# Two gate tiles of a decoder block made in the input projection instead of between attention steps

## The chip, the cores and the metric

The kernel runs on one core of a Trainium2 chip. The metric is the device time of one execution in microseconds; lower is better. A core has TensorE (PE, matmuls into the PSUM banks), VectorE (DVE), ScalarE (ACT), GpSimd (POOL) and SyncE (SP, which issues nearly all DMAs here). Each runs its own instructions in order and waits for the others by semaphores.

## The reference

One layer of a decoder trunk on x of 1024 rows and 1024 channels, all in float32. Cut to what matters:

```python
h = rms_norm(x, norm_gain, 1e-6)
proj = einsum('bsd,de->bse', h, w_in)        # 1024 x 8456
(qa, ka, va, ga, qb, kb, vb, gb, qc, kc, vc, fc, gc, gm) = split(proj)
ya = rms_norm(diff_attention(qa, ka, va, lam), subln_gain) * (1 - lam_init)   # 4 heads, all keys before
yb = sliding_window_attention(qb, kb, vb, sinks)                              # 8 heads, window 128
yc = forgetting_attention(qc, kc, vc, cumsum(log_sigmoid(fc + b_forget)))     # 8 heads, all keys before
ua, ub, uc = (y * silu(g)) @ w_up            # for each of the three branches, 512 -> 1024
gates = sigmoid(gm.reshape(B, S, 3, D))      # three gates of 1024 channels
merged = gates[:, :, 0]*ua + gates[:, :, 1]*ub + gates[:, :, 2]*uc
out = rms_norm(x + merged @ w_o, final_gain)
```

The part that the change touches is `gm`: 3 x 1024 of the projection's columns, that is 24 tiles of 128 channels by 1024 rows, eight for each branch.

## The kernel before

Every number that a matmul reads is held as a rounded part and a rest (`hi` and `lo`, function `split`, L98 to L104), and a product is three matmuls: hi by hi, hi by lo, lo by hi (`mm3`, L106 to L111). A matmul has 128 x 128 weights and 512 columns (512 rows of x). One tile of 128 output channels over 1024 rows and 1024 inputs therefore costs 8 inner blocks x 2 halves of the rows x 3 = 48 matmuls when it is made directly, and two tiles 96. `strassen` (L162 to L215) makes two tiles together from seven products of 12 matmuls, 84 in all. For that it also needs sums of the weights (`comb`, L167 to L170, DVE) and sums of the products (DVE), and four combinations of the activations, which are made once (`t_part`).

The program has these stages, in order:

1. x is normalised and transposed, and the v columns are projected.
2. The input projection proper: one direct tile (`KB`), then a list `tiles` that is taken in pairs, each pair a call of `strassen` (L503 to L511). The list holds the q and k tiles of the three branches, the tiles of the silu gates, and those tiles of `gm` that are not named in `DIRECT`: `tiles += [... sigm(bi, d)) for bi in (0, 2, 1) for d in range(NK) if (bi, d) not in DIRECT]`. Such a tile goes through the sigmoid at once (`sigm`, L440 to L445: ACT at L443, a DMA to the scratch tensor `gmd` at L444).
3. Attention, 64 steps ("units"): 16 of the window branch (b), 32 of the forgetting branch (c), 16 of the differential branch (a). The last two are taken per head in groups of two row blocks, g = 3, 2, 1, 0, from long rows to short ones. PE's order here is the order in which the code is written (`manual_schedule`); the other engines' order is set by a scheduler. In step n PE makes the scores of unit n (L755 or L630), and between them the transposes (L676) and the products with v (L709 or L780) of unit n - 2. In between, for a unit, come: on DVE the masked scores and their row minimum (L757, L650), on ACT the exponential (L760, L656), on DVE a reciprocal (L658), on POOL the scaling of the row (L664; in branch a the sum of two rows, L840). A transposed tile goes out of PSUM by ACT (L682) and DVE (L683). Scores have two PSUM buffers, so a score waits for the row minimum of the score before last.
4. Between these pieces stand the *fillers* (`fillers`, L519 to L541): the tiles of `DIRECT`, made directly, three matmuls at a time (L531 to L533; I call three a slot), 16 slots a tile. Each piece of attention work has a cost c, and behind it `fill(c * rate[kind] / 0.65)` adds to an account from which whole slots are spent; `rate` is `FILL_B`, `FILL_C` or `FILL_A` by the branch. `FILL_0 = 28` slots stand ahead of the first score, and `FILL_END = 8` are kept for the end. A filler's weights are split on POOL (L103 and L104); its result goes raw to `gmd` (L537, L538). The last six tiles of `DIRECT` are made for the second half of the rows first. Once that is done, the buffers of those rows are free, and from that step on two pieces per step of branch b's gating are put in (`gate_load`, `gate`: L560, L567, L101, L104), eight gatings in all.
5. The up-projections in the order b, c, a with the gates (`up`, L1033 to L1048). A gate tile of `DIRECT` gets its sigmoid here (L1040). Then the output projection (again by `strassen`) and the last norm.

## Time and profile before

| | |
|---|---|
| median of three runs | 1188.73 us (1188.29 to 1191.81) |
| the profiled execution | 1184.62 us, span 1182.8 us |
| PE busy in the span | 1147.9 us (97%), 5787 matmuls seen |
| PE weight loads | 972.6 us (82%) |
| DVE, ACT, POOL busy | 815.4 (69%), 585.5 (50%), 693.8 us (59%) |
| input projection (first to last matmul of it) | 129.8 to 529.5 us |
| first 28 filler slots | 529.5 to 548.6 us |
| attention, from the first score to the last product | 548.6 to 962 us |
| up- and output projection | 962 to 1182.8 us |

Busy time of PE is to be read with care: a matmul's row lasts 0.39 us, but the next one starts 0.23 us later, so rows overlap, and a PE that is always busy need not be at its full pace. The pace is read from starts, in the timeline. What an engine waited for stands in brackets behind a row of the timeline, and summed up in the view of the waits.

### The profile page before, as it was taken

The numbers are of one execution on the slowest core, as the hardware profiler recorded it, in microseconds if no ns is written. First come the engines' busy times: TensorE is split into PE (matmuls) and PEld (weight loads), VectorE is DVE, ScalarE is ACT, GpSimd is POOL, SyncE is SP. The second block draws the span as 40 slices with busy tenths as digits, with TensorE's granted clock in tenths as the row PEclk, the third lists the DMA queues.
The fourth block names the chain that finished last, engine by engine and source line by source line (L and its number), as shares of the span: only waits on it lengthen the run. The fifth ranks groups of instructions, "written<-read, shape, count | busy, mean of one in ns | idle before, by whom it ended". The sixth has DMA issues, their size and how long they took to land. (4 is left out here: it accounts for less than half of the span.)

```text
span 1182.8 us, 18767 instructions
## 1 busy us (share of the span) xinstructions
PE 1147.9 (97%) x5787; PEld 972.6 (82%) x5787; DVE 815.4 (69%) x1655; ACT 585.5 (50%) x1255; POOL 693.8 (59%) x684
## 2 busy tenths in 40 slices
PE   7999999999999999998999999999998999999997
PEld 6999888888888888887888888888877878888775
DVE  7767767768687775322887767768677835664898
ACT  6432333433444444323886666667877842334423
POOL 5056656657667676454556665766767732477643
PEclk8999999999999999999999999999999999999999
DMA  7442266666856555349946466466668359798322
GB/s 242 155 153 91 103 209 230 233 213 198 266 185 205 166 164 161 99 117 247 258 117 194 133 191 183 134 176 172 176 205 234 121 163 337 271 345 306 129 107 107
DMA packets 184531, 221.70 MB, mean 187 GB/s; under 512 B 16280, under 2 KB 116712, under 8 KB 182640
## 3 DMA queue, kind: packets, MB, share of 16 engines
q1 hardware_dynamic: 184288, 219.99, 58.9%
q8 instruction: 46, 0.75, 0.3%
q14 instruction: 53, 0.43, 0.1%
q10 hardware_dynamic: 144, 0.52, 0.1%
HBM read 144.89 MB, written 75.56 MB: 186 GB/s over the span
## 5 line engine op out<-in xcount | busy, mean ns | idle before, releaser
L104 POOL TENSOR_TENSOR w_lo<-w_st,w_hi 128x512 fp32r<-128x512 f32 x130 | 173.4, 1340 | 108.5 <-ACT w_hi L101 89.4
L104 POOL TENSOR_TENSOR w_lo<-w_sf,w_hi 128x512 fp32r<-128x512 f32 x96 | 143.2, 1494 | 104.8 <-ACT w_hi L101 84.4
L109 PE MATMUL pm<-t,w_hi 128*128 128x512 f32 x320 | 126.3, 395 | 0.7 <-ACT w_hi L101 0.7
L111 PE MATMUL pm<-t,w_lo 128*128 128x512 f32 x320 | 126.3, 395 | 0.0
L110 PE MATMUL pm<-t,w_hi 128*128 128x512 f32 x320 | 126.0, 394 | 0.0
L630 PE MATMUL sc<-qk 128*128 128x512 f32 (+2 forms) x384 | 101.9, 356 | 3.7 <-DVE m L650 3.7
L683 DVE TENSOR_TENSOR pt<-tp,pt 128x512 fp32r<-128x512 f32 x102 | 70.1, 687 | 23.8 <-ACT pt L682 23.0
L169 DVE TENSOR_TENSOR w_sf<-w_st 128x512 f32<-128x512 f32 x40 | 47.7, 1193 | 43.5 <-DMA w_st<-in_w_in_dram 34.8
L630 PEld LDWEIGHTS sc<-qk 128*128 128x128 f32 x384 | 64.6, 189 | 15.3 <-DVE m L650 6.8
L101 ACT CAST w_hi<-w_sf 128x512 fp32r<-128x512 f32 x96 | 58.5, 613 | 35.4 <-PE pm L110 29.5
L109 PEld LDWEIGHTS pm<-t,w_hi 128*128 128x128 f32 x320 | 60.1, 188 | 14.9 <-ACT w_hi L101 1.1
L110 PEld LDWEIGHTS pm<-t,w_hi 128*128 128x128 f32 x320 | 60.1, 188 | 14.1
L111 PEld LDWEIGHTS pm<-t,w_lo 128*128 128x128 f32 x320 | 60.1, 188 | 14.1
L101 ACT CAST w_hi<-w_st 128x512 fp32r<-128x512 f32 x86 | 51.3, 615 | 37.6 <-PE pm L110 28.5
L682 ACT CAST pt<-tp 128x512 fp32r<-128x512 f32 x102 | 59.4, 582 | 20.4 <-PE tp L676 18.8
L423 ACT ACTIVATE qk_hi<-u 128x512 fp32r<-128x512 f32 x32 | 20.2, 633 | 94.2 <-DVE u L191 43.9
L664 POOL TENSOR_SCALAR e_c<-e_c,r 128x1024 f32<-128x1024 f32 (+3 forms) x64 | 47.9, 749 | 23.8 <-DVE r L658 20.0
L709 PE MATMUL y<-pt,v 128*128 128x256 f32 x336 | 55.4, 290 | 2.4 <-DVE pt L683 2.2
L656 ACT ACTIVATE e_c<-e_c,m 128x1024 f32<-128x1024 f32 (+3 forms) x64 | 49.9, 780 | 13.7 <-DVE m L650 12.8
L840 POOL TENSOR_TENSOR e_a<-e_a,e_a 128x896 f32<-128x896 f32 (+7 forms) x32 | 47.3, 1481 | 15.9 <-ACT e_a L839 15.8
L656 ACT ACTIVATE e_a<-e_a,m 128x896 f32<-128x896 f32 (+7 forms) x64 | 49.6, 775 | 13.3 <-DVE m L650 13.1
L1048 POOL TENSOR_TENSOR mt<-mt,row 128x512 f32<-128x512 f32 x28 | 39.5, 1426 | 24.7 <-DVE row L1047 24.6
(299 smaller groups left out, 3511.4 us busy)
## 6 DMA issues: line engine op xcount, KB each, us to landing
w_st<-in_w_in_dram SPq DMA_DIRECT2D x126, 256.0 KB, 3.4
qk<-qd SPq DMA_DIRECT2D x224, 128.0 KB, 3.1
wo<-wod SPq DMA_DIRECT2D x14, 1024.0 KB, 9.0
row<-gmd SPq DMA_DIRECT2D x48, 256.0 KB, 4.5
qd<-qk_hi SPq DMA_DIRECT2D x42, 256.0 KB, 4.1
qd<-qk_lo SPq DMA_DIRECT2D x42, 256.0 KB, 4.9
vd<-vt SPq DMA_DIRECT2D x24, 384.0 KB, 2.3
v<-vd SPq DMA_DIRECT2D x9, 1024.0 KB, 9.8
```

The lines of the kernel that those rows point to most:

```text
L101: first = nc.scalar.copy(hi, src)
L104: return first, eng.tensor_tensor(lo, src, hi.bitcast(F32), ALU.subtract)
L109: nc.tensor.matmul(ps, w[0][:, k, :], r[0][:, k, :], start=start and k == 0, stop=False)
L110: nc.tensor.matmul(ps, w[0][:, k, :], r[1][:, k, :], start=False, stop=False)
L111: nc.tensor.matmul(ps, w[1][:, k, :], r[0][:, k, :], start=False, stop=stop and k == n - 1)
L169: nc.vector.tensor_tensor(t, x, y, op)
L630: nc.tensor.matmul(ps[:, :n], q, kk[t][c][:, o:o + n], start=t == 0, stop=t == 1)
L656: nc.scalar.activation(e[:, :L], e[:, :L], AF.Exp, bias=m2, scale=-1.0, accum_out=den)
L664: nc.gpsimd.tensor_scalar(out=e, in0=e, scalar1=r, scalar2=1.0, op0=ALU.mult, op1=ALU.mult)
L682: nc.scalar.copy(pt[:, 0, a:], tp[:, a:])
L683: nc.vector.tensor_tensor(pt[:, 1, a:], tp[:, a:], pt[:, 0, a:].bitcast(F32), ALU.subtract)
L709: nc.tensor.matmul(y[:, :256], l_, r_, start=t == 0 and n == 0, stop=last and n == len(mms) - 1)
```

## The change

```diff
-DIRECT = [(0, d) for d in range(8)] + [(2, d) for d in (6, 7, 4, 5, 2, 3, 0, 1)]
+DIRECT = [(0, d) for d in range(2, 8)] + [(2, d) for d in (6, 7, 4, 5, 2, 3, 0, 1)]
 NLAST, GPART, NY, NSUM = 6, 2, 5, 8.0
 GATE_AT = {"b": (0, 1, 2, 3, 4, 4, 5, 5), "c": (1, 1, 2, 2, 3, 4, 5, 5)}
 FILL_END, FILL_Z = 8, 1.5
-FILL_0, FILL_B, FILL_C, FILL_A = 28, 0.8, 0.6, 0.75
+FILL_0, FILL_B, FILL_C, FILL_A = 28, 0.68, 0.51, 0.64
```

Gate tiles 0 and 1 of branch a leave `DIRECT`, and so enter the list `tiles` as one more pair for `strassen`, between the silu gates and the gate tiles of branch b. There are 224 filler slots in place of 256: 28 stand ahead of the first score as before, 37 in place of 44 in branch b's steps, 81 in place of 95 in branch c's, 70 in place of 81 in branch a's, and 8 at the end as before.

On PE, at the end of the projection: `t` are the combined activations, `h` the activations, `pm` and `pj` the PSUM tiles of the projection and of a filler. Before, the 20th pair is the last one, and the fillers begin behind it:

```order
L109 MATMUL pm<-t_1313,w_hi 128x512
L110 MATMUL pm<-t_1314,w_hi 128x512
L111 MATMUL pm<-t_1313,w_lo 128x512
L531 MATMUL pj<-h01h,w_hi 128x512
L532 MATMUL pj<-h01l,w_hi 128x512
L533 MATMUL pj<-h01h,w_lo 128x512
```

and now, at the same row of PE's list:

```order
L109 MATMUL pm<-t_1313,w_hi 128x512
L110 MATMUL pm<-t_1314,w_hi 128x512
L111 MATMUL pm<-t_1313,w_lo 128x512
L109 MATMUL pm<-h00h,w_hi 128x512
L110 MATMUL pm<-h00l,w_hi 128x512
L111 MATMUL pm<-h00h,w_lo 128x512
```

A pair of 84 matmuls more stands between the last combination product and the first filler.

On PE in branch c, from the last score of the third head's g = 3 unit (the first row, `sc` of 384 columns) to its first transposes (`tp`, four of them). Before:

```order
L630 MATMUL sc<-qk 128x384 x2
L531 MATMUL pj<-h01h,w_hi 128x512
L532 MATMUL pj<-h01l,w_hi 128x512
L533 MATMUL pj<-h01h,w_lo 128x512
L630 MATMUL sc<-qk 128x512 x2
...
L630 MATMUL sc<-qk 128x256 x2
L531 MATMUL pj<-h11h,w_hi 128x512
L532 MATMUL pj<-h11l,w_hi 128x512
L533 MATMUL pj<-h11h,w_lo 128x512
L676 MATMUL tp<-ident,e_c 128x128 x4
```

and now, the end of the same stretch:

```order
L709 MATMUL y<-ptz_5170,v 128x256 x4
L630 MATMUL sc<-qk 128x256 x2
L676 MATMUL tp<-ident,e_c 128x128 x4
L531 MATMUL pj<-h00h,w_hi 128x512
L532 MATMUL pj<-h00l,w_hi 128x512
```

The slot that stood ahead of the transposes now stands behind them; in this stretch there were three slots and there are two. So it is in four of the eight heads; in the other four there were two before, and there are two.

On DVE, where branch b's gating begins (`gate` L567, `yg_b` L104) among branch a's row minima (L650). Before, behind the last unit of the second head:

```order
L650 ISA e_a_10135,m<-sc,posA 128x256
L650 ISA m 128x1
L658 RECIPROCAL r<-den 128x1
L838 COPY dens<-den 128x1
L567 TENSOR_TENSOR gate<-gate 128x512
L658 RECIPROCAL r<-den 128x1
```

and now:

```order
L683 TENSOR_TENSOR ptz_5170<-tp,ptz_5170 128x384
L658 RECIPROCAL r<-den 128x1
L837 SCALAR_TENSOR_TENSOR r<-r,nlam,den 128x1
L567 TENSOR_TENSOR gate<-gate 128x512
L683 TENSOR_TENSOR pt<-tp,pt 128x512
L650 ISA e_a_10108,m<-sc,posA 128x128
```

Counted in scores from the first step of attention, the eight gatings stood behind scores 208, 211, 218, 228, 229, 234, 238 and 249, and now stand behind 204, 205, 208, 215, 227, 228, 232 and 238.

## Rows read from the trace of the kernel before

**Rows 1.** Windows by stage: stretch, busy time of each engine (instructions), clock, DMA, GB/s

```profile
129.80:529.50 399.70, 399.05 (x1729) 324.36 (x1728) 271.18 (x311) 157.49 (x275) 253.66 (x178) 1.00 0.58 183
548.60:575.00 26.40, 22.44 (x125) 19.02 (x124) 18.02 (x71) 18.40 (x61) 12.57 (x24) 0.94 0.91 256
575.00:625.00 50.00, 50.00 (x298) 43.53 (x297) 42.29 (x143) 41.38 (x130) 28.15 (x52) 1.00 0.60 170
625.00:800.00 175.00, 173.84 (x1084) 152.96 (x1083) 123.98 (x371) 113.21 (x253) 113.28 (x186) 1.00 0.58 167
800.00:875.00 75.00, 73.85 (x436) 63.13 (x434) 54.51 (x191) 57.48 (x127) 50.02 (x49) 1.00 0.62 183
875.00:962.00 87.00, 78.74 (x469) 65.80 (x468) 59.65 (x192) 66.27 (x152) 59.69 (x58) 1.00 0.55 164
962.00:1182.80 220.80, 210.77 (x912) 171.41 (x910) 155.78 (x216) 75.16 (x145) 108.66 (x76) 0.98 0.65 230
```

**Rows 2.** Timeline of PE (start, length), first matmuls of two successive pairs in the projection

```profile
393.75 0.39 PE L109 MATMUL pm<-h00h,w_hi 128*128 128x512 f32 x1
...
413.15 0.39 PE L109 MATMUL pm<-h00h,w_hi 128*128 128x512 f32 x1
```

**Rows 3.** Timeline of PE, two filler slots in branch c and what follows each

```profile
735.20 0.39 PE L531 MATMUL pj<-h11h,w_hi 128*128 128x512 f32 x1
...
735.90 0.63 PE L709 MATMUL y<-ptz,v 128*128 128x256 f32 x4
...
737.08 0.48 PE L531 MATMUL pj<-h11h,w_hi 128*128 128x512 f32 x1
...
737.86 0.63 PE L630 MATMUL sc<-qk 128*128 128x512 f32 x2
```

**Rows 4.** Waits of PE in attention, 548.6 to 962: us in total, times, longest

```profile
PE sc L630 <- DVE m L650: 3.7, 6, 2.6
PE sc L755 <- DMA qk<-qd: 3.4, 2, 2.3
PE y L709 <- DVE pt L683: 2.2, 1, 2.2
PE pj L867 <- POOL y L104: 1.5, 2, 1.0
...
PE tp L676 <- POOL e_c L664: 0.7, 2, 0.4
```

**Rows 5.** Timeline of PE, first steps of attention

```profile
553.17 0.77 PE L755 MATMUL sc<-kb,qk 128*128 128x256 f32 x2 [2.27 <-DMA qk<-qd]
553.74 0.63 PE L531 MATMUL pj<-h10h,w_hi 128*128 128x512 f32 x1
...
555.02 1.05 PE L755 MATMUL sc<-kb,qk 128*128 128x256 f32 x4
...
557.00 0.39 PE L531 MATMUL pj<-h10h,w_hi 128*128 128x512 f32 x1
```

**Rows 6.** Timelines of PE and POOL, the third head's g = 3 unit of branch c

```profile
677.36 0.40 PE L531 MATMUL pj<-h11h,w_hi 128*128 128x512 f32 x1
...
678.06 0.60 PE L676 MATMUL tp<-ident,e_c 128*128 128x128 f32 x4
676.25 1.02 POOL L664 TENSOR_SCALAR e_c<-e_c,r 128x896 f32<-128x896 f32 x1
```

**Rows 7.** Timeline of all engines around PE's longest wait in branch a

```profile
884.45 2.52 POOL L104 TENSOR_TENSOR w_lo<-w_st,w_hi 128x512 fp32r<-128x512 f32 x2
...
884.49 1.28 DVE L837 SCALAR_TENSOR_TENSOR r<-r,nlam,den 128x1 f32<-128x1 f32 x1
...
886.15 1.37 DVE L567 TENSOR_TENSOR gate<-gate 128x512 f32<-128x512 f32 x1
...
888.19 0.73 PE L630 MATMUL sc<-qk 128*128 128x512 f32 x2 [2.62 <-DVE m L650]
```

**Rows 8.** Groups of instructions: sigmoids of the direct gate tiles in the up-projection

```profile
L1040 ACT ACTIVATE row<-row 128x512 f32<-128x512 f32 x32 | 19.9, 631 | 35.2 <-DMA row<-gmd 33.7 <-DVE w_sf L169 0.9 <-POOL w_lo L104 0.6
```

## The prediction

> **What bounds the kernel now.** I read the windows by stage first, then PE's timeline inside the two stages that the change touches, then PE's waits there, and last the other engines around the longest wait. The windows show PE busy for 399.05 of the projection's 399.70 us, while DVE is at 271, POOL at 254 and ACT at 157 [rows 1]. That busy share alone proves little, since rows overlap; the starts do: the first matmuls of two successive pairs lie 413.15 - 393.75 = 19.40 us apart [rows 2], which over 84 matmuls is 0.231 us each, the spacing of matmuls that wait for nothing. The projection is bound by PE's own work.
>
> In attention PE is again busy nearly throughout in branch c (173.84 of 175 us, DVE 71%, POOL and ACT 65%), but the others come nearer in branch b (DVE 85%, ACT 83% of 575 to 625) and in the last stretch of branch a PE drops to 78.74 of 87 us while ACT is at 76% [rows 1]. The waits name what PE waits for: 3.7 us for row minima, 3.4 for the first query rows to land, 2.2 for one transposed tile from DVE, 1.5 for a split on POOL, 0.7 for scaled rows [rows 4]. So attention is bound by PE with little to spare: the fillers are what fills the time in which the chain from a score to its transposes runs. Whether a removed slot gives its time back depends on whether that chain was already late at its place.
>
> **The change part by part.** I add up against the profiled execution (1184.62 us, of which 1182.8 is the span; the rest lies outside it). The median of three is 1188.73, 4.1 us above, and I carry the difference over to the median.
>
> *Added in the projection: one pair.* 84 matmuls, by the distance of two pairs 19.40 us [rows 2]. It brings four weight loads, four combinations and four more sums on DVE, seven operand splits on ACT and POOL, four sigmoids and four stores on SP. The average pair gets 19.4/399.7 of what these engines do in that stage: 13.2 us of DVE, 12.3 of POOL, 7.6 of ACT, and DMA is at 0.58 [rows 1]. All of it lies beside PE's 19.40; if that cover were gone, the pair would still be no longer than its longest engine, which is PE. Term: +19.4, between 19.2 and 19.8.
>
> *Removed from attention: 32 slots.* In PE's order 75 of 256 slots stand directly behind transposes, afterwards 66 of 224; so 9 of that kind leave and 23 of the other. The other kind costs 735.90 - 735.20 = 0.70 us; behind transposes it is 737.86 - 737.08 = 0.78 [rows 3], and in that row the first matmul is 0.09 longer. Sum 23 x 0.70 + 9 x 0.78 = 23.1 us, of which 7 slots lie in branch b, 14 in c, 11 in a. Full return would give 19.4 - 23.1 = -3.7 us. The 28 slots ahead of the first score and the 8 at the end stay.
>
> *What is late next, branch b.* Unit 0's last scores wait 2.27 us for query rows, and one slot follows them at 553.74 [rows 5]. In the new order it moves behind one more score, and the account pays one slot less in each of several early steps, while the first transposes wait for a chain that starts with that landing. The loads themselves stand behind the same 28 slots, so the wait for them stays. Of the 7 slots I let two bring nothing: 1.4 us lost, between 0 and 4.9 (all seven; DVE at 85% and ACT at 83% leave 15% of 75 us, so all seven could also come back).
>
> *Branch c.* The tight place is the first transposes of a g = 3 unit. In the third head POOL has scaled the second row at 676.25 + 1.02 = 677.27, and the transposes start at 678.06, after a slot that started at 677.36 [rows 6]. Without that slot they would start at 677.36, 0.09 behind POOL: the slot comes back, with nothing left over. Four of the eight heads lose a slot there, and the first transposes already wait for POOL in two places, 0.7 us together [rows 4]. I take 1 us lost of 14 x 0.72 = 10.1; ends 0 and 2.8 (a slot in each of the four).
>
> *Branch a.* The score at 888.19 waited 2.62 us, behind a row minimum that stood on DVE behind L837 (1.28 us for one column) and a gating of 1.37 [rows 7]. Where DVE is this late, taking a slot away ahead of the score only lengthens the wait. Of 11 slots I let three bring nothing, 2.2 us: the two long waits, 2.6 on a row minimum and 2.2 on a tile from DVE [rows 4], are places where a slot less can't help, and I allow for one more. Ends: 8.0 (all eleven) and -4.8, if the two longest waits of branch a (2.6 and 2.2) go, because the gatings now stand about one step earlier, at another place of DVE's queue. The row of L837 beside POOL's L104 shows a DVE instruction on one column held for the time of a POOL instruction. The Trainium skill (SBUF — State Buffer, section Who interferes with whom) says that VectorE and GpSimd share a port pair that one of them holds for a whole instruction; the trace agrees, 1.28 us against a POOL pair of 2.52. By that rule fewer filler splits on POOL make such holds rarer, which would push toward the end at -4.8; I keep it as part of the first rival.
>
> *Moved sigmoids.* Four of the 32 sigmoids in the up-projection go, 0.63 us each on ACT [rows 8]; ACT is busy 75 of 220.8 us there and PE 210.8 [rows 1], so they were hidden: 0. If they weren't, -2.5. The row sums of branch a (the waits of `pj L867`, 1.5 us) are queued by a clock that counts work times 1 + rate; they move by less than a step: 0.
>
> Sum: 19.4 - 23.1 + 1.4 + 1.0 + 2.2 = +0.9 us. From 1184.62 that is 1185.5 for an execution like the profiled one, and from the median 1188.73 it is 1189.6. The ends: 19.2 - 23.1 - 4.8 - 2.5 = -11.2 and 19.8 - 23.1 + 4.9 + 2.8 + 8.0 = +12.4.
>
> **Rivals.** *First: all slots come back and some waits go.* For it: branch c, with 14 of the 28 slots that count, has PE at 99% and the others at 65 to 71%; the gatings start earlier, where g = 0 units leave room. It gives -3.7, and with the two long waits gone -8.5: 1185.0 down to 1180.2, in the middle 1183. Against it: the waits that exist show that some places have no reserve, and a faster PE meets DVE at a new alignment that can be as bad.
>
> *Second, the other side: the chain behind the scores takes the pace over.* Its place is branch b and branch a, where a score waits for a row minimum; its price is one slot, 0.72 us, per place at which a slot is missing and the wait grows by as much. It decides from 7.3 us lost on, that is ten of the 32 slots not given back: then the sum is over +3.6. With 12 lost it is +4.9, 1193.6; with 16, +7.8, 1196.5. For it: DVE and ACT at 83 to 85% in branch b and ACT at 76% in branch a beside a PE that isn't full. Against it: in branch b no wait on DVE or ACT stands among the long ones of [rows 4], and in c they would have to rise from 71% to over 75% only.
>
> *Third, slower by the clock.* After the waits for the query rows, the slot at 553.74 took until 555.02, 1.28 us in place of 0.70, and up to 557.00 PE needed 3.83 us for ten score matmuls and a slot, about 1.9 us of work at the usual spacing; the granted clock of that stretch is 0.94 [rows 5, 1], a part of it at the lower level of 1.2 GHz. The Trainium skill (TensorE: Matmul & The Clock Gate, section HAM oscillation — how this bites in real kernels) says that waits between bursts of matmuls let the clock fall; the trace agrees at the start of attention, but behind the 2.62 us wait at 888 the stretch 875 to 962 still has 1.00 [rows 1, 7]. A longer wait in branch a would cost about 1.9 us a fall; two of them on top of my sum are +4.7, 1193.4. I count this with the second rival.
>
> That the slots don't leave is excluded by PE's order, which has 12 matmuls fewer and 96 filler matmuls less.
>
> **How the numbers follow.** A measurement of this kernel can tell a change of about 0.3%, 3.6 us, from none: faster means below 1185.2, slower above 1192.3. My case, between them, with its middle at 1189.6: 0.60. The first rival reaches below 1185.2 in part of its range: 0.15. The second and third: 0.25, more than the first because full return itself stops just at the bound and everything beyond needs waits to vanish, while ten lost slots need only places like those seen. The range that holds the time 8 times in 10 cuts the far ends: 1184 (full return and a quarter of the long waits gone) to 1195.5 (14 slots lost).
>
> **What would show it.** In the profile after: the pair appears as 19.4 us more between the first projected tile and the first filler, with the fillers starting near 549; if that stage grows by more than 20, the cover by DVE and POOL was wrong. Attention, from the first score to the last product, now 413 us, should take about 395 (413 - 23.1 + 4.6); 390 or less speaks for the first rival, 398 or more for the second. The waits of scores on row minima should grow from 4 to 6 us; if they stay, the losses that I put into branch a were wrong, and if the scaled rows (`tp` on POOL) grow past 3 us, branch c was tighter than I took it. The stage from 962 on should keep its 220.8. A clock below 1.00 in a stretch of branch a speaks for the third.

## The result, and the profile after

The change makes the kernel slower: 1202.76 us (median of four runs, 1201.46 to 1205.73) against 1188.51 (1188.05 to 1191.81) for the kernel before on the same chip, a ratio of 1.0127, 95% interval 1.0102 to 1.0153. The forecast was 1189.6, from 1184 to 1195.5; the time lies above that range. The profiled execution has a span of 1199.7 us, 16.9 more than before; by the medians it is 14.3 more, so 2.6 us belong to the two executions that were profiled.

The same stages as in [rows 1], cut at the same instructions. The first table is put together from the starts of PE's instructions in the two traces; "slots' worth" is the number of removed slots times 0.72 us, the mean of [rows 3].

| us | before | after | change | slots' worth | not given back |
|---|---|---|---|---|---|
| ahead of the projection | 129.8 | 128.4 | -1.4 | | |
| projection | 399.8 | 419.2 | +19.4 | | |
| 28 slots ahead | 19.1 | 19.1 | 0 | | |
| branch b | 76.6 | 76.7 | +0.1 | -5.1 (7) | 5.2 |
| branch c | 174.2 | 167.4 | -6.8 | -10.1 (14) | 3.3 |
| branch a | 162.2 | 166.2 | +4.0 | -7.9 (11) | 11.9 |
| the rest | 221.2 | 222.8 | +1.6 | | |
| span | 1182.8 | 1199.7 | +16.9 | -23.1 | 20.4 |

The pair costs what was said, to the tenth. Of the 23.1 us of removed slots 20.4 do not come back (about 18 by the medians), where the forecast took 4.6. How the 20.4 divide over the branches hangs on the one execution of before; the experiment with the pair alone, below, has the old order a second time. The windows by stage of the kernel after (stretch, busy time of each engine with instructions, clock, DMA share, GB/s; branch a in two pieces, as before):

```profile
128.40:547.60 419.20, 418.54 (x1814) 340.04 (x1813) 283.59 (x322) 165.14 (x287) 261.53 (x185) 1.00 0.57 180
...
566.60:643.40 76.80, 70.61 (x402) 59.68 (x401) 58.26 (x213) 59.78 (x187) 39.62 (x75) 0.96 0.68 188
643.40:810.70 167.30, 163.31 (x1037) 144.01 (x1036) 124.95 (x371) 113.19 (x254) 111.64 (x185) 1.00 0.60 171
810.70:880.40 69.70, 66.24 (x398) 56.68 (x397) 53.17 (x182) 53.80 (x119) 44.70 (x42) 1.00 0.61 185
880.40:977.00 96.60, 83.77 (x475) 68.52 (x473) 64.01 (x203) 69.20 (x159) 59.84 (x60) 0.96 0.49 143
977.00:1199.70 222.70, 210.05 (x913) 170.58 (x913) 155.18 (x216) 72.53 (x140) 108.02 (x76) 0.99 0.64 230
```

PE is less full: 70.61 of 76.8 us in branch b (72.44 of 76.4 before), 83.77 of 96.6 in the last stretch of branch a (78.74 of 87.0), whose clock is now 0.96 (1.00 before, [rows 1]). PE's waits in attention after (us in total, times, longest), which answer to [rows 4]:

```profile
PE sc L630 <- DVE m L650: 6.6, 7, 3.0
PE tp L676 <- POOL e_c L664: 3.9, 7, 1.0
PE tp L676 <- POOL eb L664: 3.6, 1, 3.6
PE pj L867 <- ACT ya L868: 2.5, 2, 2.0
PE pj L867 <- ACT gr L537: 2.4, 1, 2.4
```

Each branch has its own row. **Branch b** has one new wait of 3.6 us for a scaled row `eb` on POOL. The timeline of all engines after, at that place:

```profile
601.03 0.54 SPq L799 DMA_DIRECT2D ck<-cd  x1
...
601.66 0.18 DVE L768 RECIPROCAL r<-d 128x4 f32<-128x4 f32 x1
...
606.58 1.12 POOL L802 TENSOR_SCALAR dk<-ck 128x1024 f32<-128x1024 f32 x1 [5.65 <-DMA ck<-cd]
607.67 1.85 POOL L664 TENSOR_SCALAR eb<-eb,r 128x256 f32<-128x256 f32 x4
608.21 1.84 PE L676 MATMUL tp<-ident,eb 128*128 128x128 f32 x4 [3.58 <-POOL eb L664]
...
610.14 0.59 ACT L682 CAST pt<-tp 128x512 fp32r<-128x512 f32 x1 [4.24 <-PE tp L676]
...
611.79 0.48 DVE L757 CUSTOM_DVE_ANT_0 eb<-sc,posB,nsink 128x256 f32<-128x256 f32 x1 [6.24 <-PE sc L755]
```

The reader is to see a queue that stands: POOL's next instruction is branch c's first decay row `dk`, which needs `ck`, a transfer issued at 601.03. POOL stands idle for it for 5.65 us. The four scalings of branch b behind it need nothing from `ck`: their reciprocal, the row at 601.66, was done at 601.84. But POOL takes its instructions in order, so they start 5.8 us after that, and PE, ACT and DVE wait one behind the other. In the kernel before, `dk` stands behind that unit's scalings, and its transfer was issued 6.2 us ahead of it. POOL's and SP's timelines before:

```profile
585.38 0.55 SPq L799 DMA_DIRECT2D ck<-cd  x1
588.75 1.84 POOL L664 TENSOR_SCALAR eb<-eb,r 128x256 f32<-128x256 f32 x4 [0.40 <-DVE r L768]
591.61 1.12 POOL L802 TENSOR_SCALAR dk<-ck 128x1024 f32<-128x1024 f32 x1 [1.02 <-DMA ck<-cd]
```

There the four scalings stand ahead of `dk`, afterwards behind it: with PE's order moved by a few slots, the scheduler changed their places on POOL. PE's granted clock is 0.67 over these 8 us, part of them at the lower level of 1.2 GHz. The window after:

```profile
604.00:612.00 8.00, 4.42 (x15) 2.96 (x14) 1.72 (x9) 2.53 (x8) 5.34 (x12) 0.67 0.49 136
```

**Branch c** has the wait of transposes for `e_c` on POOL, 0.7 us in two places before [rows 4] and 3.9 in seven after: 3.2 us more, about the 3.3 that it does not give back. **Branch a** loses most. Its heads, from first score to first score, and slots in each:

| head | before | after | slots before, after |
|---|---|---|---|
| first | 34.3 | 33.7 | 21, 18 |
| second | 37.9 | 36.0 | 22, 18 |
| third | 42.0 | 46.5 | 22, 19 |
| fourth | 48.0 | 50.0 | 24, 23 |

The third and fourth, where most of branch b's gatings stand, grow although they have fewer slots. The timeline after, at the first of two bad places in the third head:

```profile
878.63 0.46 SPq L560 DMA_DIRECT2D gate<-yd_b  x1
...
879.18 5.91 SPq L608 DMA_DIRECT2D qk<-qd  x9
...
884.11 1.54 DVE L567 TENSOR_TENSOR gate<-gate 128x512 f32<-128x512 f32 x1 [2.50 <-DMA gate<-yd_b]
885.58 0.68 DVE L650 CUSTOM_DVE_ANT_0 e_a<-sc,posA 128x512 f32<-128x512 f32 x1
885.69 0.62 ACT L101 CAST yg_b<-gate 128x512 fp32r<-128x512 f32 x1 [3.55 <-DVE gate L567]
...
886.32 0.96 PE L630 MATMUL sc<-qk 128*128 128x512 f32 x2 [3.04 <-DVE m L650]
```

It is the same picture as on POOL. DVE's next instruction is a gating's product, whose load was issued at 878.63, just ahead of nine loads of the next head's q and k; it starts at 884.11. Behind it stands the masked score with its row minimum (885.58), behind that PE's next score; ACT stands in the same way before the gating's rounding, with a copy of transposes behind it. PE waits 3.04 us. The second place, further on in the same timeline:

```profile
907.48 4.59 SPq L608 DMA_DIRECT2D qk<-qd  x7
...
912.88 0.33 SPq L560 DMA_DIRECT2D gate<-yd_b  x1
...
913.88 0.56 PE L867 MATMUL pj<-y,ones 128*2 128x256 f32 x2 [2.38 <-ACT gr L537]
...
916.94 0.69 DVE L567 TENSOR_TENSOR gate<-gate 128x512 f32<-128x512 f32 x1 [3.34 <-DMA gate<-yd_b]
```

Here the gating's load is issued behind seven loads and DVE starts its product 4.1 us later, having stood for 3.34. But PE's wait of 2.38 us is not behind it: it ended at 913.88, three us before the product, and was for a copy `gr` on ACT, which itself stood behind an exponential whose row minimum DVE gave at 912.5. The score that follows the product starts without a wait. So only the first place shows late data reaching PE; how the second hangs together with the loads these rows do not show. At each place the clock falls. Windows of the kernel after:

```profile
884.00:888.00 4.00, 1.68 (x7) 1.25 (x8) 3.89 (x9) 1.85 (x4) 1.26 (x2) 0.83 0.51 145
888.00:892.00 4.00, 4.00 (x19) 3.44 (x19) 2.35 (x9) 2.50 (x6) 1.19 (x2) 0.74 0.47 153
892.00:912.00 20.00, 17.24 (x97) 13.90 (x95) 17.36 (x52) 16.25 (x33) 14.09 (x11) 1.00 0.63 190
912.00:916.00 4.00, 2.12 (x10) 1.96 (x11) 0.73 (x4) 2.33 (x7) 2.30 (x3) 0.74 1.05 261
916.00:920.00 4.00, 4.00 (x24) 3.34 (x23) 2.51 (x4) 2.06 (x5) 1.98 (x3) 0.83 0.72 208
```

From 884 to 892 the granted clock is 0.83 and 0.74 in the two halves, from 912 to 920 it is 0.74 and 0.83, part of each at the lower level of 1.2 GHz. That is 4 x (0.26 + 0.17) = 1.7 us of PE time at each place, where the forecast had taken about 1.9 a fall. DVE's wait for `yd_b` in branch a is 7.6 us in four places, 3.2 in four before.

### The profile page after: what moved, and what is told of

Read it like the earlier page. It is cut to its first block, busy times and chain, and to the rows that moved or that the text cites. A ratio compares the mean times of both kernels' runs of the same rounds, so it can differ in the third digit from the quotient of the medians.

```text
span 1199.7 us, 18797 instructions
## 1 busy us (share of the span) xinstructions
PE 1150.7 (96%) x5775; PEld 970.4 (81%) x5775; DVE 829.7 (69%) x1666; ACT 589.8 (49%) x1259; POOL 693.3 (58%) x683
## 5 line engine op out<-in xcount | busy, mean ns | idle before, releaser
L104 POOL TENSOR_TENSOR w_lo<-w_st,w_hi 128x512 fp32r<-128x512 f32 x129 | 171.7, 1337 | 117.0 <-ACT w_hi L101 98.4
L104 POOL TENSOR_TENSOR w_lo<-w_sf,w_hi 128x512 fp32r<-128x512 f32 x100 | 146.3, 1466 | 113.6 <-ACT w_hi L101 104.5
L109 PE MATMUL pm<-t,w_hi 128*128 128x512 f32 x336 | 132.6, 395 | 0.7 <-ACT w_hi L101 0.7
L111 PE MATMUL pm<-t,w_lo 128*128 128x512 f32 x336 | 132.6, 395 | 0.0
L110 PE MATMUL pm<-t,w_hi 128*128 128x512 f32 x336 | 132.3, 394 | 0.0
L630 PE MATMUL sc<-qk 128*128 128x512 f32 (+2 forms) x384 | 104.5, 361 | 6.7 <-DVE m L650 6.6
L169 DVE TENSOR_TENSOR w_sf<-w_st 128x512 f32<-128x512 f32 x42 | 51.6, 1229 | 45.0 <-DMA w_st<-in_w_in_dram 34.2
L101 ACT CAST w_hi<-w_sf 128x512 fp32r<-128x512 f32 x100 | 61.0, 613 | 38.5 <-PE pm L110 31.9
L630 PEld LDWEIGHTS sc<-qk 128*128 128x128 f32 x384 | 64.2, 190 | 18.0 <-DVE m L650 10.3
L109 PEld LDWEIGHTS pm<-t,w_hi 128*128 128x128 f32 x336 | 63.1, 188 | 15.6 <-ACT w_hi L101 1.1
L110 PEld LDWEIGHTS pm<-t,w_hi 128*128 128x128 f32 x336 | 63.1, 188 | 14.9
L111 PEld LDWEIGHTS pm<-t,w_lo 128*128 128x128 f32 x336 | 63.0, 188 | 14.9
L656 ACT ACTIVATE e_c<-e_c,m 128x1024 f32<-128x1024 f32 (+3 forms) x64 | 49.9, 779 | 9.9 <-DVE m L650 6.5
```

Source lines behind the costliest of these rows:

```text
L101: first = nc.scalar.copy(hi, src)
L104: return first, eng.tensor_tensor(lo, src, hi.bitcast(F32), ALU.subtract)
L109: nc.tensor.matmul(ps, w[0][:, k, :], r[0][:, k, :], start=start and k == 0, stop=False)
L110: nc.tensor.matmul(ps, w[0][:, k, :], r[1][:, k, :], start=False, stop=False)
L111: nc.tensor.matmul(ps, w[1][:, k, :], r[0][:, k, :], start=False, stop=stop and k == n - 1)
L169: nc.vector.tensor_tensor(t, x, y, op)
```

## The experiments

Eighteen kernels were run. Stages are read from one profiled execution each; times and ratios are medians of several runs against the kernel before on the same chip. How far a stage moves by itself can be read from the old order, which ran twice: branch a takes 162.2 us (before) and 164.6 (the pair alone, next), branch b 76.6 and 73.9. So a difference of 2 to 3 us between two executions proves nothing of its own. In the experiments line numbers have moved by a few. Where the first expectations use letters, Q is the theory of a changed order in a queue (`dk` on POOL, the gatings' first step), S that of row sums asked for too early.

**The pair alone.** The kernel before, with the two tiles made in the projection as well (and still as fillers):

```diff
-                      if (bi, d) not in DIRECT]
+                      if (bi, d) not in DIRECT or (bi, d) in ((0, 0), (0, 1))]
```

> The kernel before with one pair more in the input projection: gate tiles 0 and 1 of branch a are made there AND by the fillers (the up-projection still reads what the fillers wrote), so the 256 slots and the order of attention stay. Both theories: the projection grows by 19.4 us (19.2 to 19.8) and the whole by the same, 1208 us; attention from the first score stays at 413 us and the last stage at 220 us. If the whole grows by more than 21 us, the pair costs more than its 84 matmuls and my term for it was wrong.

1204.94 against 1185.94 us, ratio 1.0161 (1.0143 to 1.0179), which is +19.0. The projection takes 419.2 us. The term of the pair is right, and nothing else hides in it.

Attention has the old order here, so this is a second execution of it. Branch b takes 73.9 us, branch c 174.9, branch a 164.6, its heads 34.3, 37.3, 45.1 and 47.9. In branch b the kernel before had waited 3.4 us for query rows, with a fall of the clock behind it; this one waits 0.9, at a clock of 1.00. Branch a has two falls of the clock here, after PE waits of 2.27 and 2.58 us. Measured against this execution, 7.9, 2.6 and 9.5 us do not come back in branches b, c and a, in place of 5.2, 3.3 and 11.9. The sum is 20.0 instead of 20.4, but the third head of branch a grows by 1.4 us only, and two falls of the clock in branch a are no mark of the change.

**Undoing the swap on POOL, and starting the gatings later.** The first kernel is the changed one with an edge that holds the first `dk` back until unit 12's scalings are issued; the second starts the gatings at step 56 as before the change (55 in the changed kernel); the third does both:

```diff
+                first = ExitStack()
+                if h == 0 and g == 3:
+                    first.enter_context(tc.issue_after(scaled[4 * 12 + 3].ins))
...
-            if "free" in cur:
+            if "free" in cur and n >= 56:
```

> The changed kernel, with branch c's first decay row on GpSimd (L802, which waits for the DMA of ck) issued behind the scaling of unit 12 of branch b in place of ahead of that of unit 7. Theory Q (heads of queues): the 7 us hole at 606 to 613 us and the low clock behind it go; branch b takes 70 to 72 us in place of 76.8, the whole 1196 to 1198 in place of 1202.8. Theory D (density: the chain behind the scores has no reserve, so a missing slot is not given back anywhere): branch b finds other waits and stays within 1 us of 76.8, the whole at 1201 to 1204.

> The changed kernel, with branch b's gating starting at step 56 as in the kernel before, one step later than in the changed one. Theory Q: DVE no longer stands 2.5 us for the gating's load ahead of a row minimum; the third head of branch a (46.5 us in the changed kernel, 42.1 before) comes back to 40 to 43, the whole to 1196 to 1199. Theory D: the third head stays at 45 to 47 us, since the waits there come from the missing slots, and the whole stays within 1.5 us of 1202.8.

> Both edits together. Theory Q: the gains add, 10 to 12 us, 1191 to 1193. Theory D: 1200 to 1204.

The swap alone: 1196.80 us, ratio 1.0096 (1.0075 to 1.0116), down from 1.0127; branch b takes 70.5 us in place of 76.7, branch c 167.3, branch a 166.5. So the standing queue cost branch b 6.2 us, and the medians say the same (1202.76 - 1196.80 = 6.0). POOL now scales where PE needs it, and no wait of PE for `eb` is left. How much of the seven slots' 5.1 us then comes back depends on what it is held against: 6.1 us against the 76.6 of the kernel before, 3.4 against the 73.9 of the same order with the pair alone. POOL's and PE's timeline of this kernel, at the same unit:

```profile
604.00 0.54 SPq L801 DMA_DIRECT2D ck<-cd  x1
604.10 1.84 POOL L664 TENSOR_SCALAR eb<-eb,r 128x256 f32<-128x256 f32 x4 [1.09 <-DVE r L770]
604.48 0.60 PE L676 MATMUL tp<-ident,eb 128*128 128x128 f32 x4
```

The gatings' first step alone: 1202.63 us, ratio 1.0144 (1.0124 to 1.0163), branch a 169.9, third head 47.2. That theory fell: at the old step, and with fewer slots, DVE still waits 4.0 us for a gating's load (at 919.80) and the third head is as long. Both: 1196.49, ratio 1.0083 (1.0063 to 1.0104), branch a 166.3. All later kernels have the swap undone; I call that kernel the mended one.

**Row sums, and where the slots are.** Four variants of the mended kernel: the clock that queues branch a's row sums at its old speed; and three distributions of the 224 slots over b, c, a: 37, 70, 81 (branch a as before), 37, 95, 56 (branch c as before), 44, 95, 49 (all old rates, the account then runs dry in branch a's third head).

```diff
-                tick(c * (1 + rate[kind]))
+                tick(c * (1 + {"b": 0.8, "c": 0.6, "a": 0.75}[kind]))
...
-FILL_0, FILL_B, FILL_C, FILL_A = 28, 0.68, 0.51, 0.64
+FILL_0, FILL_B, FILL_C, FILL_A = 28, 0.68, 0.44, 0.75
...
+FILL_0, FILL_B, FILL_C, FILL_A = 28, 0.68, 0.6, 0.52
...
+FILL_0, FILL_B, FILL_C, FILL_A = 28, 0.8, 0.6, 0.75
```

> dk_late (the changed kernel with the first decay row issued later, 1196.8 us; its branch a took 166.5 us) with the clock that places branch a's row sums (L867 of the changed kernel) counting with the old rates, so that the sums stand nearly where they stood before the change. Theory S (the sums' new places): the two long waits of the sums, 2.3 us for the copy of a filler's result and 2.6 for that of a sum, go, and branch a takes 159 to 163 us. Theory D (in branch a the other engines set the pace, so a missing slot gives nothing back, wherever the sums stand): branch a stays at 164 to 168 us.

> dk_late with the slots dealt out anew, still 224: branch a gets back the old rate 0.75 and all its 81 slots, branch c pays (rate 0.44, 70 slots in place of 81, and 95 before the change). Theory D: branch a takes 162 us as before the change, not longer than with 70 slots (166); in branch c the first transposes of the g = 3 units wait longer for POOL, 6 us or more in all, and it takes 162 us or more in place of the 159.4 that eleven more slots given back would leave of 167.3. Full return: branch a 174, branch c 159.4.

> dk_late with branch c at its old rate 0.6 and 95 slots, and branch a paying (rate 0.52, 56 slots in place of 70). Theory D: branch c 174 us again with 0.7 us of waits for POOL; branch a stays at 163 to 168 us although it has 14 slots (10 us) less, so the whole is 5 to 8 us slower than dk_late. Full return: branch a 156 us, the whole as dk_late within 3 us.

> dk_late with all three old rates, 0.8, 0.6 and 0.75: the 224 slots go at the old density until they run out in the third unit of branch a's third head; the later units have none but the last 8. Theory D: branch b 75 to 77 us, branch c 174, branch a's first two heads 34 and 37 to 38 us as before the change, its last two heads not shorter than 88 us together (90 before with 45 slots), the whole 1208 or more. Full return: the last two heads 24 slots, 17 us, shorter than before the change, 73 us, the whole 1190 to 1195.

| kernel | us | ratio | b | c | a | heads of a |
|---|---|---|---|---|---|---|
| row-sum clock | 1196.41 | 1.0088 (1.0060 to 1.0116) | 71.7 | 167.4 | 164.9 | 33.7, 38.3, 44.0, 49.0 |
| 37, 70, 81 | 1187.80 | 1.0018 (1.0000 to 1.0036) | 71.2 | 162.7 | 163.6 | 34.3, 37.3, 43.3, 48.7 |
| 37, 95, 56 | 1211.48 | 1.0212 (1.0188 to 1.0236) | 69.9 | 177.0 | 177.4 | 32.3, 50.8, 47.3, 46.9 |
| 44, 95, 49 | 1208.05 | 1.0183 (1.0159 to 1.0207) | 73.8 | 175.3 | 164.8 | 38.4, 49.9, 33.0, 43.4 |

The row sums were not it: their waits stayed (3.2 and 2.1 us, 2.6 and 2.3 in the mended kernel), and branch a is 1.6 us shorter, less than the 2.4 between two executions of the old order. The slots' place matters more than their number. With the same 224 slots the time goes from 1187.80 to 1211.48 us. Branch a with 81 slots is 2.9 us shorter than the mended one with 70, and with 56 it is 10.9 longer. Branch c gives 4.6 more for 11 slots less (worth 7.9). Where the fillers of the last `DIRECT` tiles end earlier, the gatings start earlier (step 50 with all old rates, 53 with 56 slots in branch a), and the long head is then the second: 49.9 us with 22 slots, against 37.3 with 22 where the gatings are not in it. So the cost follows the gatings. PE's waits with 56 slots, branch a:

```profile
PE pj L873 <- ACT gr L537: 15.7, 2, 9.0
PE sc L630 <- DVE m L650: 7.3, 5, 3.0
```

The 9.0 us are the picture of the first bad place again: DVE's gating waits 5.0 us for its load, ACT stands 4.2 us before the gating's rounding (at 881.67), and behind that stands the copy `gr` (883.05) that PE's row sum needs.

**Branch c: the row on POOL in two pieces.** In the mended kernel and in the one with 81 slots, each of the two rows of a g = 3 unit is scaled in two halves. The thought was that the transposes could begin after the first half:

```diff
-                normalise(e[:, :n], r)
+                if g == 3:
+                    normalise(e[:, :512], r)
+                    normalise(e[:, 512:n], r)
+                else:
+                    normalise(e[:, :n], r)
```

> Branch c's rows of a g = 3 unit (1024 columns) are scaled on POOL in two halves, so that the first transposes wait for the first half alone; the rest is as in dk_late (branch c there 167.3 us, seven heads with a wait of transposes on POOL, 3.8 us together). Theory POOL row: that wait is what branch c does not give back; it falls under 1 us, branch c comes to 163.5 to 164.5, and the whole is about 3 us shorter than dk_late. Rival, density: in branch c PE is full apart from that and the wait only takes another place (on ACT's copies or the exponential); branch c stays at 166 to 168. A third outcome: the eight more instructions on POOL cost more than they bring, branch c over 168.

> a_full (37 slots in branch b, 70 in c, 81 in a; branch c 162.7, branch a 163.6) with the scaling in two halves. Theory POOL row: the wait of transposes on POOL, 2.8 us there, goes, branch c 160 to 161 and the whole 2 to 3 us shorter than a_full, which would put it at or just under the kernel before. Rival: no change, branch c 162 to 164.

1196.45 us, ratio 1.0080 (1.0052 to 1.0108), branch c 166.7 in place of 167.3; and 1187.28, ratio 1.0008 (0.9985 to 1.0031), branch c 161.2 in place of 162.7. PE's wait for `e_c` in the first, in place of 3.8 us:

```profile
PE tp L676 <- POOL e_c L664: 3.2, 7, 0.9
```

This does not price the scaling. The transposes need a half of both rows, and POOL is not done earlier. POOL and PE at one of the seven places in the mended kernel:

```profile
687.25 0.70 POOL L807 TENSOR_SCALAR dk<-ck 128x512 f32<-128x512 f32 x1 [1.78 <-DVE r L658]
687.91 1.12 POOL L664 TENSOR_SCALAR e_c<-e_c,r 128x1024 f32<-128x1024 f32 x1
...
689.26 1.02 POOL L664 TENSOR_SCALAR e_c<-e_c,r 128x896 f32<-128x896 f32 x1
...
690.34 0.66 PE L676 MATMUL tp<-ident,e_c 128*128 128x128 f32 x4 [0.38 <-POOL e_c L664]
```

and with the halves:

```profile
686.25 0.70 POOL L807 TENSOR_SCALAR dk<-ck 128x512 f32<-128x512 f32 x1 [1.77 <-DVE r L658]
686.91 1.38 POOL L664 TENSOR_SCALAR e_c<-e_c,r 128x512 f32<-128x512 f32 x2
...
688.51 1.27 POOL L664 TENSOR_SCALAR e_c<-e_c,r 128x512 f32<-128x512 f32 x2
689.27 0.66 PE L676 MATMUL tp<-ident,e_c 128*128 128x128 f32 x4 [0.30 <-POOL e_c L664]
```

From the start of `dk` to the transposes it is 3.09 us in the first and 3.02 in the second. What the rows do show is the link that holds PE here: from the reciprocal of the first row on, POOL works without a gap, and the transposes start as it ends. Among its work is `dk` of the next unit, 0.70 us and so longer than the wait of 0.38, and it stands ahead of both scalings at the seven heads that wait. In the kernel before it stands behind the first of the two at seven of eight heads. So a change of order on POOL is a candidate here too, beside the missing slots. No run moved `dk` at these places, and which of the two it is stays open.

**Branch a without gatings.** The mended kernel (70 slots) and the one with 81, with the gatings of branch b put off until attention is over (`if "free" in cur and n >= 999`).

> dk_late with no gating of branch b between the steps of branch a (all of it after attention); 70 slots in branch a. Theory gating: the gatings on DVE and POOL are what eats the removed slots of branch a; without them branch a falls from 166.5 to about 155, about 8 us under nogate81, and the last stage grows by the gatings that come late. Rival, the score chain: branch a is set by the chain from a score over DVE, ACT and POOL back to PE, with or without gatings; it stays above 161 and within 3 us of nogate81.

> a_full with no gating between the steps of branch a, 81 slots in branch a. Theory gating: branch a hardly changes from 163.6 (160 to 164), since 81 slots cover what the gatings hold up, and is about 8 us longer than in nogate70. Rival, the score chain: both kernels have about the same branch a, whatever its slots.

1190.06 us, ratio 1.0029 (1.0010 to 1.0047), and 1185.44, ratio 0.9988 (0.9968 to 1.0007). In both, the first up-projection then waits for the late gatings; this wait of PE with 70 slots:

```profile
PE p L109 <- ACT yg_b L101: 8.1, 1, 8.1
```

The heads of branch a are 33.8, 35.8, 36.3 and 55.6 us with 70 slots (the last with the 8.1 in it), 34.3, 37.5, 38.2 and 54.0 with 81 (with 8.2). So with the gatings in it the third head is 10.3 us longer with 70 slots and 5.1 with 81. Neither theory was right by itself: the gatings do take that time, but without them eleven slots fewer are still worth only 161.5 - 8.1 against 164.0 - 8.2, that is 2.4 of 7.9 us, from one execution of each.

**Late data or work?** First with the gatings' loads issued one piece further ahead, then with the gatings moved into the fourth head (three pieces a step), each with 70 and with 81 slots:

```diff
-        gq = [gb[0][0]] + [f for n in range(8) for f in ([gb[n + 1][0]] if n < 7 else []) + [gb[n][1]]]
+        gq = [gb[0][0], gb[1][0]] + [f for n in range(8) for f in ([gb[n + 2][0]] if n < 6 else []) + [gb[n][1]]]
...
-NLAST, GPART, NY, NSUM = 6, 2, 5, 8.0
+NLAST, GPART, NY, NSUM = 6, 3, 5, 8.0
...
-            if "free" in cur:
+            if "free" in cur and n >= 60:
```

> dk_late (70 slots in branch a, branch a 166.5 us, third head 46.6) with the gatings' data loaded one piece further ahead, so that each product on DVE comes a step after its load. Theory late data: in the third head the loads of the next head's q, k and v crowd the gatings' loads, DVE's product stands at the head of its queue and waits for them (6.9 us for yd_b in all), the row minima wait behind it and PE behind those; here that wait falls under 2 us, the third head to 38 to 42 us, no stretch of branch a stays under clock 0.9, and the whole is 5 to 8 us shorter than dk_late. Rival, work: the gatings' own time on DVE, ACT and POOL is what costs; the third head stays at 45 to 48.

> The same in a_full (81 slots in branch a, third head 43.3 us, wait of DVE for yd_b 2.7). Theory late data: little to gain, 41 to 43 us in the third head. Rival, work: no change. If ahead70 gains and ahead81 doesn't, the removed slots of the third head had been what covered the late data.

> dk_late with the gatings begun in the first step of the fourth head (step 60 of 64, three pieces a step), where no head's data are loaded any more. Theory late data: the third head is as without gatings, 36 to 37 us (46.6 in dk_late); the fourth stays within 2 us of 50, so that branch a comes to 156 to 158 and the whole is 8 to 10 us shorter than dk_late. Rival, work: what the third head saves the fourth loses, and branch a stays at 163 or more.

> The same in a_full. Theory late data: third head 38 us (43.3 in a_full), fourth within 2 us of 49, the whole 3 to 5 us shorter than a_full, below the kernel before. Rival, work: the fourth head takes 4 to 5 us more, and the whole stays level with a_full. By either theory, late70 against late81 says what eleven slots of branch a are worth without late data: 2 us by the heads of nogate70 and nogate81, 8 if they come back.

| kernel | us | ratio | a | third and fourth head |
|---|---|---|---|---|
| loads ahead, 70 | 1197.84 | 1.0102 (1.0079 to 1.0125) | 166.9 | 47.3, 49.9 |
| loads ahead, 81 | 1188.27 | 1.0019 (0.9996 to 1.0043) | 163.8 | 44.5, 47.8 |
| fourth head, 70 | 1194.06 | 1.0069 (1.0048 to 1.0089) | 162.3 | 36.2, 56.2 |
| fourth head, 81 | 1187.69 | 1.0020 (1.0004 to 1.0036) | 167.7 | 38.2, 57.7 |

Neither told the two apart. With the loads ahead DVE still waited 5.5 us for `yd_b` (6.9 in the mended kernel), so the suspected cause had not been taken away; in the fourth head the price came back there (6.3 and 9.0 us), which spoke for work. So in the last two the work stays and the loads go: the factors come from a tile that is in SBUF. These two kernels leave branch b's true gating out, and their result is not the reference's; only their times are of use.

```diff
+        if br == "b":
+            return [cur["row"][0].tile([P, 512], F32, name="gate", tag=cur["row"][1], bufs=cur["row"][2])]
...
-        nc.vector.tensor_tensor(yt, yt, ts[1], ALU.mult)
+        if br == "b":
+            nc.vector.tensor_tensor(yt, cur["pos"][:, :512], cur["pos"][:, 256:768], ALU.mult)
```

> dk_late in which the gatings of branch b take their two factors from a tile that is in SBUF already, so that nothing is loaded for them (branch b's part of the output is not the reference's); the same instructions on DVE and ACT at the same steps. Without gatings the third and fourth head take 36.3 and 47.5 us, with them 46.6 and 49.9. Theory work: the gatings' instructions are what costs; third head 44 to 47, branch a 163 or more. Rival, late data: DVE's queue standing before loads is what costs; third head 36 to 39, no clock fall there, branch a 155 to 158, the whole 8 to 11 us shorter than dk_late. Between 40 and 43 both have a part.

> The same in a_full (third head 43.3 us with gatings, 38.2 without). Theory work: third head 42 to 44. Rival, late data: 38 to 39.5. With nodata70 this also gives what eleven slots of branch a are worth when the gatings' data are never late: about 8 us if all come back, 2.4 as without gatings.

With 70 slots: 1188.30 us, ratio 1.0023 (1.0001 to 1.0045), down from 1.0096. The third head takes 36.7 us (46.6), the fourth 51.6, branch a 158.2 (166.5). With 81: 1182.33 us, ratio 0.9988 (0.9963 to 1.0013); third head 37.7 (43.3), fourth 50.9, branch a 160.2 (163.6). DVE's timeline with 70 slots, where the gatings are:

```profile
880.40 0.69 DVE L570 TENSOR_TENSOR gate<-posA 128x512 f32<-128x512 f32 x1
...
893.86 1.12 DVE L570 TENSOR_TENSOR gate<-posA 128x512 f32<-128x512 f32 x1
```

and its windows over most of the third and of the fourth head:

```profile
884.00:920.00 36.00, 33.71 (x204) 28.32 (x203) 30.93 (x95) 28.39 (x67) 29.21 (x26) 1.00 0.50 150
920.00:960.00 40.00, 35.31 (x214) 28.81 (x212) 26.85 (x81) 29.87 (x72) 25.75 (x25) 1.00 0.21 67
```

About the same work runs in the third head (four of the eight gatings, as in the mended kernel), none of it waits for a load, the clock stays at 1.00, and 10 us are gone; by the medians of the whole kernel it is 8.5. In the third head it was the loads and not the work. By which way is shown at the first of the two bad places alone, where the late data stand at the head of DVE's and ACT's queues. The loads also take room on SP, on the DMA engines and in buffers, and the scheduler may set instructions a little differently without them; these runs do not part the one from the other. In the fourth head the work itself costs: 51.6 and 50.9 us here are no less than with the loads, against 47.5 and 45.8 without gatings (55.6 - 8.1 and 54.0 - 8.2).

No version is faster than the kernel before beyond what the runs can tell. The best that computes everything, 81 slots in branch a without gatings between its steps, has 0.9988 with an interval across 1.

## Why the prediction was wrong

The term +19.4 for the pair held: 419.2 - 399.8 = 19.4. The step that failed is the sum of what does not come back of the 23.1 us of removed slots, 1.4 + 1.0 + 2.2 = 4.6 in the forecast, 20.4 measured (about 18 by the medians). By its parts:

- **Branch b, "Of the 7 slots I let two bring nothing": 1.4 taken, 5.2 measured.** The reason was wrong as well as the size. I looked for the loss at the query rows, whose wait is 3.4 us before, 1.4 after and 0.9 in the old order's second execution, so it moves from one execution to the next with the slots unchanged. The loss lay on POOL, in a swap of `dk` and four scalings, which costs 6.2 us by itself. The order of POOL before and after could be read, and the trace of before shows `dk` already waiting 1.02 us for its data; I read the orders only on PE and DVE.
- **Branch c, 1.0 taken, 3.3 measured (2.6 against the old order's second execution).** The place was right (the first transposes of a g = 3 unit, behind POOL). But seven heads wait there, and the forecast had found a slot less ahead of the transposes in four only, so the missing slot cannot be the whole of it. The forecast's own sign, the wait of `tp` on POOL past 3 us, has come: 3.9. What makes the other heads wait stays open.
- **Branch a, "Of 11 slots I let three bring nothing": 2.2 taken, 11.9 measured (9.5 against the second execution), over the end of 8.0.** Three parts, from the runs with and without loads. First, eleven slots are worth 160.2 - 158.2 = 2.0 of 7.9 us even where the gatings have no loads, and 2.4 without gatings; without the loads PE waits 11.4 us in branch a with 70 slots and 6.5 with 81, so it waits for the chain in most of the time that the slots had filled (5.9 lost). By the medians of the whole kernel even these 2 us are not to be seen. Second, the gatings' loads cost 166.5 - 158.2 = 8.3 us with 70 slots and 163.6 - 160.2 = 3.4 with 81 (4.9 more). What is left, some 1 us, is within what branch a moves by itself. The forecast let three slots bring nothing where about eight do, and priced the gating in [rows 7] by its 1.37 us of work and not by its load. That DVE already stood 3.2 us before the gatings' `yd_b` in the kernel before was in its waits. An earlier first step is not what made it worse, since the old step with fewer slots is no better (47.2 us for the third head). That leaves the fewer slots around the gatings.
- **Sigmoids, 0, and the last stage:** it went from 221.2 to 222.8 us, and from 219 to 225 in other kernels with the same code there. Nothing shown.

The second rival, by which the chain behind the scores takes the pace over, came true at one of its two places, branch a, and it was given its share of 0.25 together with the third, whose falls of the clock came too, two in branch a (as many as in the old order's second execution) and one in branch b. But the price per place was wrong: I set one slot, 0.72 us, so that even 16 lost slots gave 1196.5. (The end of 1195.5, called 14 lost slots, is 1195.1 by the same sum.) A removed slot cannot cost more than itself if all else stays; here all else did not stay. On POOL `dk` came to the head of the queue ahead of work that PE needed, and cost 6.2 us, more than eight slots' worth. On DVE and ACT the gatings had stood at the head of the queue before the change too; with fewer slots around them their loads cost 4.9 us more.

By the signs named ahead: the projection grew by 19.4 (right); attention took 410.3 us from first score to the up-projection, against a bound of 398 that spoke for the second rival; waits on row minima grew from 3.7 to 6.6 us (4 to 6 named); clock 0.96 in the last stretch of branch a, the sign of the third rival, which the old order's falls weaken.

The Trainium skill (SBUF — State Buffer, Who interferes with whom), on which the forecast drew for its first rival, says that VectorE and GpSimd share ports that one of them holds for a whole instruction. That fewer filler splits on POOL mean fewer such holds was the forecast's own step, and it did not come true. The one-column instruction of [rows 7], all 32 of it (us in total, mean in ns), before and after:

```profile
L837 DVE SCALAR_TENSOR_TENSOR r<-r,nlam,den 128x1 f32<-128x1 f32 x32 | 13.4, 418 | 0.8
L837 DVE SCALAR_TENSOR_TENSOR r<-r,nlam,den 128x1 f32<-128x1 f32 x32 | 17.5, 547 | 0.7
```

It takes longer with fewer splits, and ACT's waits for it grow from 4.6 us to 8.2. No run takes POOL's part away, so how much of this is the shared ports, and what it costs PE, is not shown.

The Trainium skill's other page (TensorE: Matmul & The Clock Gate, HAM oscillation — how this bites in real kernels) says that waits between bursts of matmuls let the clock fall. That agrees with the new rows: after PE waits of 3.04, 2.38 and 3.58 us the granted clock falls to 0.74 or less in a stretch of 4 to 8 us. The wait's length alone does not decide, since 2.62 us in the kernel before left it at 1.00 [rows 1, 7] and 2.27 us with the pair alone did not.

## What to carry to other kernels

A filler that is taken out gives its time back only where PE sets the pace at that place; ask for each removed slot which engine's instruction comes next, and count the places where that one is already late. When PE's order changes and a scheduler orders the rest, read the other engines' queues too, and look for instructions that wait for a transfer and have moved ahead of something PE needs: such an instruction is priced by the landing of its data, not by its length. To tell a load from work, leave the work and take the load away; moving either told little here. And have the old order run a second time before a stage is priced: here branch b moved by 2.7 us and branch a by 2.4 between two executions of one order.

## What the runs showed of the hardware that was not expected

A load issued beside many others came late: 256 KB for a gating were issued 0.55 us ahead of nine loads for the next head's q and k, and the reader that stood waiting for them started 5.5 us after the issue (878.63 to 884.11). Two other such loads between 860 and 930 us have their landing in the trace, 2.8 and 3.2 us after the issue. By what the loads delay each other is not shown. And one standing queue reaches every engine: 5.65 us on POOL became 3.58 on PE, 4.24 on ACT and 6.24 on DVE, with PE's clock at 0.67 over 8 us behind it.
